# One decoder step: low parts of w_o and of two up pairs by an adding DMA, and two padding PSUM tiles

## The chip, the cores and the metric

The kernel runs on one core of a Trainium2 chip. The metric is the device time of one execution in microseconds (us); lower is better. The kernel before takes 888.28 us (median of 3 runs, 888.14 to 888.34).

## The reference

One layer of a decoder on two groups of tokens, 512 new ones and 8 sequences of 8, so 576 tokens of width 1024, all in float32:

```python
xn = rms_norm(h, g_mix)
z = xn @ w_in                      # 1024 x 6144: b, c, hc, v, gate_a, gate_b
ya = gated_short_conv(b, c, hc) @ w_out_conv
yb = multiscale_pool(v) @ w_pool * pool_scale    # 4 groups, windows 2, 4, 8, 16
h = h + (gate_a * ya + gate_b * yb) @ w_o
hn = rms_norm(h, g_mlp)
h = h + square(relu(hn @ w_up)) @ w_down         # 1024 -> 4096 -> 1024
gp = sigmoid(rms_norm(h, g_ple) @ w_ple_gate)
h = h + gp * (p @ w_ple_proj)
y = rms_norm(h, g_final)
```

It also returns the last rows of the convolution's and of the pooling's input.

## The kernel before, in words

**Precision.** Every operand of a matmul is split in two float32r tiles: `hi`, the value rounded, and `lo`, what is left. A product of two operands is three matmuls: hi by hi, lo by hi and hi by lo (`mm`, line 104, and `quarter`, line 382). The usual split (`split`, line 87) takes one ScalarE operation for `hi` (line 93) and one VectorE operation, value minus `hi`, for `lo` (line 94).

**Weights.** A weight comes in parts of 128 x 512, 256 KB each. SyncE's queue loads a part into one of 8 `raw` tiles (`raw_tile`, line 126). Its `hi` and `lo` go to the pool `wsp`, which has NF = 7 slots for each, so a part can be split when the part seven places ahead of it has been multiplied. One list, `order`, holds all parts in the order of use, and `Stream.take` keeps loads about 6 parts ahead of the splits and splits up to 7 parts ahead of TensorE. A part of w_o or of the pooling is used by 24 matmuls, a quarter of an up pair by 12.

**Adding parts.** A `Part` made with `adding=True` gets its low part in another way (lines 140 to 149): ScalarE writes `hi` (line 145), ScalarE writes `lo` = -`hi` (line 146), and GpSimd's queue issues a DMA that loads the same weight once more and adds it to `lo` (line 147). Before the change that is so for the parts of w_in and w_pool in the last three pooling groups, 16 parts in all.

**Up pairs.** The products of w_in and w_up with 512 by 512 corners are done in pairs of output blocks, with seven products of quarters where eight would be plain. A pair's eight entries in the list are the forms a, s2, s0, s1, b, (a of the next pair), d, s3. The quarters a, b and d are loaded as they are. The sums need more DMAs on GpSimd's queue: for s1 and s0 a loaded `raw` tile gets a second quarter added to it by a DMA (line 164), which first waits for the load. s2 is a sum on VectorE (line 184) of s1's tile and a; s3 another (line 186) with b. Both are issued in VectorE's stream, so VectorE stops there until the DMA of line 164 has landed.

**Stages around the change.** (1) Pooling, lines 662 to 733: for group 3, 2, 1, 0 two products of 48 matmuls, window sums on VectorE (lines 694 to 724), a split, and one group later `merge` (line 673): two products of 24 matmuls, `t` = PSUM x scale x gate (line 679), plus the mixer's other branch (line 681), a split into `merged`. (2) w_o, lines 748 to 765: eight products of 48 matmuls; the first two are opened together by `two_products` and take the groups' results in the order 2 to 7, then 0 and 1. Each product is added to x (line 755), scaled (line 758), and after every second one `hg.add` makes differences (lines 429 to 432) and splits. (3) The first up block: its first pair is opened late: four quarters run over three of the four operands (36 matmuls) while the last operand is still made, and the rest follows. Then come the pairs 1, 2 and 3.

**PSUM.** In the pooling `psump` has 4 tiles of two banks (line 664). As built, the 16 products take the banks 0-1, 6-7, 4-5, 2-3 in turn, so the last merge's two products lie in 4-5 and 2-3. The pool `banks` that follows (line 743) has 6 tiles of one bank and hands them out first as 0, 5, 4, 3, 2, 1: the first w_o product takes banks 0 and 5. With `reuse_waits="tile"` a tile waits only for those older tiles whose bytes it takes. The banks are handed out while the planner runs, from a list of free ones, so a tile more can shift who gets which.

**Order.** In stages 2 and 3 the matmuls are kept in the order of the program (`pinned`). All other engines' instructions are ordered by a planner, which plays the program through with its own costs and on each engine issues what is ready and comes first in the program. Once built, each engine's queue is fixed: an instruction that waits holds up all behind it, on GpSimd's queue DMA issues and additions of squares (line 329) alike.

Of the kernel before, what the change touches and what calls it, by code (L numbers as in the profile page):

```python
# [7 lines left out]
F32 = mybir.dt.float32  # L8
F32R = mybir.dt.float32r
AF = mybir.ActivationFunctionType  # L10
ALU = mybir.AluOpType

P = 128
D = 1024
NJ = D // P
# [3 lines left out]
NH = 2  # L19
# [17 lines left out]
KH = D // 2  # L37
NQ = NJ // 2
# [4 lines left out]
def tile_hybrid_step(ctx: ExitStack, tc: tile.TileContext, x, pt, vecs, rc, ident, sconv, spool, w_first, w_in,  # L43
                     w_pool, w_oc, w_o, w_up, w_down, w_pg, w_pp,
                     y_out, ncp, npp, ncs, nps):
    nc = tc.nc
# [5 lines left out]
    wsp = ctx.enter_context(tc.tile_pool(name="wsp", bufs=NF))  # L52
# [8 lines left out]
    psum = pool("psumx", 1, space=bass.MemoryType.PSUM)  # L61
# [21 lines left out]
    def as32(ap):  # L83
        return ap.bitcast(F32)
# [41 lines left out]
    def raw_tile(ap):  # L126
        raw = wraw.tile([P, KH], F32, tag="raw", name="raw")
        nc.sync.dma_start(raw, ap)
        return raw

    class Part:

        def __init__(self, ap, resident=False, adding=False):
            self.ap, self.resident, self.adding = ap, resident, adding
# [3 lines left out]

        def split(self):
            if self.adding:  # L140

                n = self.ap.shape[1]
                hi = wsp.tile([P, KH], F32R, tag="w", name="hi")[:, :n]
                lo = wsp.tile([P, KH], F32R, tag="wl", name="lo")[:, :n]
                nc.scalar.copy(hi, self.raw[:, :n])
                nc.scalar.mul(lo, as32(hi), -1.0)
                nc.gpsimd.dma_start(lo, self.ap, accum_op=ALU.add)
                self.raw = None
                return hi, lo
            pool, tag = (acts, "act") if self.resident else (wsp, "w")  # L150
            w = split(self.raw, [P, KH], pool, tag)
            self.raw = None
            return w
# [11 lines left out]
            return raw  # L165

    class Form:
        def __init__(self, pair, name):
            self.pair, self.name = pair, name

        def load(self):
            p, name = self.pair, self.name
# [6 lines left out]

        def split(self):  # L180
            p, name = self.pair, self.name
            if name == "s2":
                p.rs2 = tmp.tile([P, KH], F32, tag="s", name="s2", bufs=2)
                nc.vector.tensor_tensor(out=p.rs2, in0=p.rs1, in1=p.ra, op=ALU.add)  # L184
            elif name == "s3":
                nc.vector.scalar_tensor_tensor(
                    out=p.rs2, in0=p.rs2, scalar=-1.0, in1=p.rb, op0=ALU.mult, op1=ALU.subtract)
            return split(p.rs2 if name == "s3" else getattr(p, "r" + name), [P, KH], wsp, "w")
# [30 lines left out]
    def unit(ap, adding=False):  # L219
        return [Part(ap[:, i:i + KH], adding=adding) for i in range(0, ap.shape[1], KH)]  # L220

    order = []
    order += unit(w_in[NJ + NQ]) + unit(w_in[2 * NJ + NQ]) + unit(w_in[NQ])

    def forms(pairs, between=(), after=()):

        out = [Form(pairs[0], "a")]
        for q, p in enumerate(pairs):
            out += [Form(p, n) for n in ("s2", "s0", "s1", "b")]
            out += [Form(pairs[q + 1], "a")] if q + 1 < len(pairs) else list(between)  # L230
            out += [Form(p, n) for n in ("d", "s3")]
        return out + list(after)

    for q in range(1, NQ):
# [9 lines left out]
        order += unit(w_pool[g + 1], True) if g < 3 else []  # L244
    halved = [i + h * NQ for i in range(NQ) for h in range(2)]
    for j in halved:
        order += unit(w_o[j])
    for b in range(NFB):
        order += forms([Pair(w_up[b * NJ + q], w_up[b * NJ + NQ + q]) for q in range(NQ)])
        for j in range(NJ):  # L250
            order += unit(w_down[b * NJ + j])
    for i in range(2):
# [14 lines left out]
    for j in range(NJ):  # L267
# [4 lines left out]
        raw = wraw.tile([P, KH], F32, tag="raw", name="fraw")  # L272
# [17 lines left out]
    for j in range(NJ):  # L290
        if j == 0:
            hi, lo = (acts.tile([P, NH, HT], F32R, tag="act", name=n) for n in ("hi", "lo"))
            for h in range(NH):
                nc.scalar.mul(hi[:, h], xs[j][:, h], v(G_MIX, j))
                nc.vector.scalar_tensor_tensor(
                    out=lo[:, h], in0=xs[j][:, h], scalar=v(G_MIX, j), in1=as32(hi[:, h]),
# [218 lines left out]
    for u in range(3):  # L515
        for k in (NJ - 2, NJ - 1):
            first_step(k, u)
            if u == 1:
                r = stat.spread(range(3 * (k - NJ + 2), 3 * (k - NJ + 3)))
# [128 lines left out]
    gates, where, tag = mix, keep, "keep"  # L648
    pairs_of(NQ, xo, corner, finish)
    for j in range(NJ):  # L650
        ps = product(stream.take(2), ya_in)
# [3 lines left out]
    gates, where, tag = [None] * NJ, acts, "act"  # L655
# [7 lines left out]
    tmp = pool("tmpp", 8)  # L663
    psum = pool("psump", 4, space=bass.MemoryType.PSUM)
    banks = None
    sp = tmp.tile([P, NJ, DB, PB], F32, tag="sp", name="sp", bufs=1)
    nc.sync.dma_start(sp, spool)
    npp_t = tmp.tile([P, NJ, PB], F32, tag="npp", name="npp_t", bufs=1)
# [16 lines left out]
    for g, w in reversed(list(enumerate(WINDOWS))):  # L685
        pooled = []
        for i in range(2):
            j = 2 * g + i
            ps = product(stream.take(2), xg)
# [5 lines left out]
                out=e[:, PB:PE_].rearrange("p (h t) -> p h t", h=NH),  # L695
                in0=prompt(ps), in1=prompt(r1), op=ALU.mult)
            nc.vector.tensor_tensor(
                out=es[:, :, PB:].rearrange("p (h b) t -> p h b t", h=NH),
# [3 lines left out]
            s, d = e, 1  # L702
            while d < w:
                q = tmp.tile([P, PEXT], F32, tag="ext", bufs=4, name="q")
                lo = 2 * d - 1
                nc.vector.tensor_tensor(  # L706
                    out=q[:, lo:], in0=s[:, lo:], in1=s[:, lo - d:PEXT - d], op=ALU.add)
                s, d = q, 2 * d
            pl = tmp.tile([P, NH, HT], F32, tag="t", name="pl")
            nc.vector.scalar_tensor_tensor(  # L710
                out=prompt(pl), in0=s[:, PB:PE_].rearrange("p (h t) -> p h t", h=NH),
# [3 lines left out]
                out=sample(pl),  # L715
# [9 lines left out]
                out=pl[:, 0, :f], in0=head[:, :f], in1=e[:, PB:PB + f], op=ALU.subtract)  # L725
# [18 lines left out]
    psum = pool("psumm", 1, space=bass.MemoryType.PSUM)  # L744
# [7 lines left out]
    for x, j in enumerate(halved):  # L752
        ps = opened[x] if x < 2 else product(stream.take(2), merged)
# [14 lines left out]
    for b in range(NFB):  # L768
# [29 lines left out]
        for j in range(NJ):  # L798
            if j == 0:
                two = two_products(sq, halved)  # L800
            if j < 2:
                ps = two[j]
            else:
                ps = product(stream.take(2), sq)
# [158 lines left out]
```

## Time and profile before

| | us |
|---|---|
| median of 3 runs | 888.28 |
| the profiled execution | 886.94 |
| its span, first to last instruction | 885.1 |
| TensorE busy | 867.9 (98%) |
| VectorE busy | 594.1 (67%) |
| ScalarE busy | 426.5 (48%) |
| GpSimd busy | 139.5 (16%) |

The mean granted clock is 0.994 of full speed; it is 1.00 in all stretches around the change. A row of a timeline gives start, duration, engine, line, operation, what is written and read, how many instructions of a kind are merged, and in brackets the engine's idle time before it with what ended it. Matmuls overlap in the timeline: each shows about 0.29 us, while the next starts about 0.13 us after it. A matmul's start is therefore the better clock.

### The profile page before, as it was taken

The numbers are of one execution on the slowest core, as the hardware profiler recorded it, in microseconds if no ns is written. First come the engines' busy times: TensorE is split into PE (matmuls) and PEld (weight loads), VectorE is DVE, ScalarE is ACT, GpSimd is POOL, SyncE is SP. The second block draws the span as 40 slices with busy tenths as digits, with TensorE's granted clock in tenths as the row PEclk, the third lists the DMA queues.
The fourth block names the chain that finished last, engine by engine and source line by source line (L and its number), as shares of the span: only waits on it lengthen the run. The fifth ranks groups of instructions, "written<-read, shape, count | busy, mean of one in ns | idle before, by whom it ended". The sixth has DMA issues, their size and how long they took to land.

```text
span 885.1 us, 16776 instructions
## 1 busy us (share of the span) xinstructions
PE 867.9 (98%) x6506; PEld 863.5 (98%) x6506; DVE 594.1 (67%) x1063; ACT 426.5 (48%) x754; POOL 139.5 (16%) x176
## 2 busy tenths in 40 slices
PE   8999999999999999999899999999999999999995
PEld 8999999999999999899899999999999999999995
DVE  7997797974358599768873248535763377687454
ACT  8653343652135555355674247512762167546332
POOL 4212112100010242032200010011001010021353
PEclk9999999999999999999999999999999999999997
DMA  8636546644454776554444454254544454323012
GB/s 261 155 113 148 132 131 159 154 131 116 103 130 133 194 160 134 179 132 107 121 154 116 104 135 128 96 139 101 144 132 117 107 135 132 96 85 108 1 38 71
DMA packets 62160, 111.25 MB, mean 126 GB/s; under 512 B 7296, under 2 KB 11008, under 8 KB 62080
## 3 DMA queue, kind: packets, MB, share of 16 engines
q1 hardware_dynamic: 50992, 90.21, 32.0%
q0 software_dynamic: 10944, 19.93, 14.4%
q8 instruction: 51, 0.84, 0.4%
q14 instruction: 29, 0.24, 0.1%
q10 hardware_dynamic: 144, 0.03, 0.0%
HBM read 107.16 MB, written 2.99 MB: 124 GB/s over the span
## 4 chain that ended last, share of the span: by engine, by line
PE 84%; DVE 9%; issue 3%; DMA 2%; ACT 1%; SPq 0%; POOL 0%; DVEq 0%; POOLq 0%; ACTq 0%
PE b L67 76%; PE psg L67 6%; DVE lo L94 2%; DVE q L706 2%; DMA raw<-w_up 2%; PE psn L340 1%; DMA xin<-x 1%; PE psn L367 1%; ACT hi L93 1%; DVE pl L710 1%; DVE t L679 1%; DVE e L694 0%; DVE t L681 0%; PE ps L67 0%; DVE xall L755 0%
## 5 line engine op out<-in xcount | busy, mean ns | idle before, releaser
L67 PE MATMUL b<-hi 128*128 128x288 f32 x1832 | 461.9, 296 | 4.3 <-DVE t L679 1.6
L67 PE MATMUL b<-lo,hi 128*128 128x288 f32 x1832 | 460.4, 295 | 1.2 <-DVE lo L94 1.1
L67 PE MATMUL b<-hi,lo 128*128 128x288 f32 x1832 | 460.6, 295 | 0.6 <-DVE lo L94 0.6
L67 PEld LDWEIGHTS b<-hi 128*128 128x128 f32 x1832 | 317.6, 188 | 6.7 <-DVE t L679 1.8
L67 PEld LDWEIGHTS b<-lo,hi 128*128 128x128 f32 x1832 | 317.6, 188 | 1.8 <-DVE lo L94 1.6
L67 PEld LDWEIGHTS b<-hi,lo 128*128 128x128 f32 x1832 | 317.5, 188 | 0.9 <-DVE lo L94 0.8
L93 ACT CAST hi<-raw 128x512 fp32r<-128x512 f32 x288 | 177.0, 621 | 266.3 <-PE b L67 253.8
L94 DVE TENSOR_TENSOR lo<-raw,hi 128x512 fp32r<-128x512 f32 x288 | 202.8, 708 | 102.4 <-ACT hi L93 98.2
L164 POOL DMA_DIRECT2D raw<-w_up x32 | 28.1, 878 | 334.5 <-DMA raw<-w_up 151.7
L329 POOL TENSOR_TENSOR sq<-sq 128x576 f32<-128x576 f32 (+2 forms) x32 | 41.6, 1301 | 112.1 <-ACT sq L323 63.4
L93 ACT CAST hi<-s 128x512 fp32r<-128x512 f32 x60 | 37.0, 618 | 45.9 <-PE b L67 41.3
L94 DVE TENSOR_TENSOR lo<-s,hi 128x512 fp32r<-128x512 f32 x60 | 41.2, 688 | 20.3 <-ACT hi L93 18.9
L164 POOL DMA_DIRECT2D raw<-w_in x28 | 24.4, 870 | 183.7 <-DVE lo L94 71.5
L184 DVE TENSOR_TENSOR s<-raw 128x512 f32<-128x512 f32 x30 | 20.7, 690 | 45.5 <-DMA raw<-w_up 28.9
L67 PE MATMUL psg<-hi 128*128 128x320 f32 (+1 forms) x128 | 38.1, 298 | 0.0
L67 PE MATMUL psg<-lo,hi 128*128 128x320 f32 (+1 forms) x128 | 37.9, 296 | 0.0
L67 PE MATMUL psg<-hi,lo 128*128 128x320 f32 (+1 forms) x128 | 37.9, 296 | 0.0
L67 PE MATMUL ps<-lo,hi 128*128 128x288 f32 x160 | 34.4, 296 | 0.0
L67 PE MATMUL ps<-hi 128*128 128x288 f32 x160 | 34.2, 296 | 0.1
L67 PE MATMUL ps<-hi,lo 128*128 128x288 f32 x160 | 34.2, 296 | 0.0
L94 DVE TENSOR_TENSOR lo<-g,hi 128x576 fp32r<-128x576 f32 x32 | 26.3, 834 | 6.6 <-ACT hi L93 6.6
L811 DVE TENSOR_TENSOR acc<-b,acc 128x288 f32<-128x288 f32 x48 | 19.8, 450 | 15.1 <-PE b L67 15.1
(132 smaller groups left out, 803.4 us busy)
## 6 DMA issues: line engine op xcount, KB each, us to landing
raw<-w_in SPq DMA_DIRECT2D x104, 256.0 KB, 3.0
raw<-w_up SPq DMA_DIRECT2D x80, 256.0 KB, 2.9
raw<-w_down SPq DMA_DIRECT2D x64, 256.0 KB, 2.9
raw<-w_up POOLq DMA_DIRECT2D x32, 256.0 KB, 4.3
raw<-w_in POOLq DMA_DIRECT2D x28, 256.0 KB, 4.6
raw<-w_oc SPq DMA_DIRECT2D x16, 256.0 KB, 2.8
raw<-w_o SPq DMA_DIRECT2D x16, 256.0 KB, 3.5
raw<-w_pg SPq DMA_DIRECT2D x16, 256.0 KB, 2.9
```

The lines of the kernel that those rows point to most:

```text
L67: i = nc.tensor.matmul(*args, **kw)
L93: nc.scalar.copy(hi, src)
L94: nc.vector.tensor_tensor(out=lo, in0=src, in1=as32(hi), op=ALU.subtract)
L164: nc.gpsimd.dma_start(raw, y, accum_op=ALU.add)
L184: nc.vector.tensor_tensor(out=p.rs2, in0=p.rs1, in1=p.ra, op=ALU.add)
L329: nc.gpsimd.tensor_tensor(out=self.parts[0], in0=self.parts[0], in1=sq, op=ALU.add)
L340: nc.tensor.matmul(sums[:, i:i + 1], a[:, h, c:c + m], ones32[:, 0:1], start=k == 0, stop=k == len(self.parts) - 1)
L367: nc.tensor.matmul(self.ps[:, h, c:c + m], self.y[:, i:i + 1].broadcast_to([m, P]), idt[:m, :m], start=True, stop=True)
L679: nc.vector.scalar_tensor_tensor(out=t, in0=halves(ps), scalar=v(P_SCALE, j), in1=gates[j], op0=ALU.mult, op1=ALU.mult)
L706: nc.vector.tensor_tensor(out=q[:, lo:], in0=s[:, lo:], in1=s[:, lo - d:PEXT - d], op=ALU.add)
L710: nc.vector.scalar_tensor_tensor(out=prompt(pl), in0=s[:, PB:PE_].rearrange("p (h t) -> p h t", h=NH), scalar=1.0 / w, in1=e[:, PB:PE_].re ...
L811: nc.vector.tensor_tensor(out=accs[j][:, h], in0=ps[h], in1=accs[j][:, h], op=ALU.add)
```

## The change

The adding split becomes a function, `split_adding`, and serves more weights: all 16 parts of w_o, and of the first up block's pairs 0 and 1 the quarters a, b and d, 6 in all. And the pooling allocates two PSUM tiles ahead of its first product; VectorE writes one column into each.

```diff
+    def split_adding(raw, ap):
+        n = ap.shape[1]
+        hi = wsp.tile([P, KH], F32R, tag="w", name="hi")[:, :n]
+        lo = wsp.tile([P, KH], F32R, tag="wl", name="lo")[:, :n]
+        nc.scalar.copy(hi, raw[:, :n])
+        nc.scalar.mul(lo, as32(hi), -1.0)
+        nc.gpsimd.dma_start(lo, ap, accum_op=ALU.add)
+        return hi, lo
...
     class Form:
...
         def split(self):
             p, name = self.pair, self.name
+            if self.adding and name in ("a", "b", "d"):
+                return split_adding(getattr(p, "r" + name), getattr(p, name))
...
-    def forms(pairs, between=(), after=()):
+    def forms(pairs, between=(), after=(), adding=0):
-        out = [Form(pairs[0], "a")]
+        out = [Form(pairs[0], "a", adding > 0)]
         for q, p in enumerate(pairs):
-            out += [Form(p, n) for n in ("s2", "s0", "s1", "b")]
+            out += [Form(p, n, q < adding) for n in ("s2", "s0", "s1", "b")]
...
     for j in halved:
-        order += unit(w_o[j])
+        order += unit(w_o[j], True)
     for b in range(NFB):
-        order += forms([Pair(w_up[b * NJ + q], w_up[b * NJ + NQ + q]) for q in range(NQ)])
+        order += forms([Pair(w_up[b * NJ + q], w_up[b * NJ + NQ + q]) for q in range(NQ)], adding=0 if b else 2)
...
     psum = pool("psump", 4, space=bass.MemoryType.PSUM)
     banks = None
+    for _ in range(2):
+        nc.vector.memset(psum.tile([P, NH, 512], F32, tag="ps", name="pad")[:, 0, :1], 0.0)
```

## Rows read from the trace of the kernel before

**Rows 1.** The page's first part: busy time of each engine, share of the span, instructions.

```profile
PE 867.9 (98%) x6506; PEld 863.5 (98%) x6506; DVE 594.1 (67%) x1063; ACT 426.5 (48%) x754; POOL 139.5 (16%) x176
```

**Rows 2.** The chain of waits in order of time: start, us, what. One long stretch of matmuls without a stall.

```profile
456.21 354.39 PE b L67 x2664
```

**Rows 3.** Stretches: from:to, length, then busy us (instructions) of PE, PEld, DVE, ACT, POOL, granted clock, DMA share, GB/s. Most of the pooling, its end, w_o, and the first up pairs.

```profile
300.00:340.00 40.00, 40.00 (x302) 40.00 (x302) 31.72 (x58) 21.21 (x42) 14.74 (x23) 1.00 0.86 184
344.00:363.00 19.00, 17.32 (x125) 16.40 (x124) 18.82 (x37) 8.90 (x17) 0.00 (x0) 1.00 0.34 103
361.00:414.00 53.00, 51.42 (x383) 51.21 (x384) 38.67 (x60) 24.62 (x42) 11.54 (x10) 1.00 0.47 133
414.00:441.00 27.00, 24.21 (x172) 22.73 (x171) 22.60 (x39) 18.98 (x34) 5.89 (x5) 1.00 0.51 133
```

**Rows 4.** The timeline of TensorE where the pooling's last merge (ps) gives way to w_o (b).

```profile
358.36 0.43 PE L67 MATMUL ps<-hi,lo 128*128 128x288 f32 x2
358.85 0.79 PE L67 MATMUL ps<-hi 128*128 128x288 f32 x4
359.64 0.53 PE L67 MATMUL ps<-lo,hi 128*128 128x288 f32 x2
360.01 0.42 PE L67 MATMUL ps<-hi,lo 128*128 128x288 f32 x2
360.27 0.42 PE L67 MATMUL ps<-lo,hi 128*128 128x288 f32 x2
360.53 0.43 PE L67 MATMUL ps<-hi,lo 128*128 128x288 f32 x2
361.01 0.40 PE L67 MATMUL b<-hi 128*128 128x288 f32 x1
362.98 0.41 PE L67 MATMUL b<-hi 128*128 128x288 f32 x1 [1.56 <-DVE t L679]
```

**Rows 5.** The timeline of TensorE in the first up pair, when the last operand is due. Ten matmuls start from 418.79 to 422.00.

```profile
418.79 0.29 PE L67 MATMUL b<-hi,lo 128*128 128x288 f32 x1
...
419.96 0.40 PE L67 MATMUL b<-lo,hi 128*128 128x288 f32 x1 [0.40 <-DVE lo L94]
...
421.37 0.40 PE L67 MATMUL b<-lo,hi 128*128 128x288 f32 x1 [0.75 <-DVE lo L94]
...
422.74 0.40 PE L67 MATMUL b<-hi 128*128 128x288 f32 x1 [0.45 <-ACT g L441]
...
424.31 0.29 PE L67 MATMUL b<-hi,lo 128*128 128x288 f32 x1
```

**Rows 6.** The timeline of TensorE between the pairs 1 and 2. Thirteen matmuls start from 437.64 to 439.93.

```profile
437.64 0.29 PE L67 MATMUL b<-hi,lo 128*128 128x288 f32 x1
438.38 0.37 PE L67 MATMUL b<-hi 128*128 128x288 f32 x1 [0.45 <-DVE g L463]
...
440.88 0.37 PE L67 MATMUL b<-hi 128*128 128x288 f32 x1 [0.66 <-ACT hi L93]
```

**Rows 7.** The timeline of VectorE at the end of the pooling. `lo<-raw,hi` are low parts of w_o.

```profile
354.87 0.68 DVE L94 TENSOR_TENSOR lo<-raw,hi 128x512 fp32r<-128x512 f32 x1
...
360.84 0.68 DVE L94 TENSOR_TENSOR lo<-raw,hi 128x512 fp32r<-128x512 f32 x1
361.44 0.75 DVE L94 TENSOR_TENSOR lo<-t,hi 128x576 fp32r<-128x576 f32 x1
362.11 0.81 DVE L679 SCALAR_TENSOR_TENSOR t<-ps,vec,ga 128x576 f32<-128x576 f32 x1
```

**Rows 8.** The timeline of VectorE from w_o to the third up pair. L184 is the sum s2, L755 adds a w_o product to x; the `lo<-raw,hi` at 414.69 and 416.18 are those of b of pair 0 and of a of pair 1.

```profile
395.88 0.69 DVE L184 TENSOR_TENSOR s<-raw 128x512 f32<-128x512 f32 x1 [5.59 <-DMA raw<-w_up]
...
414.69 0.68 DVE L94 TENSOR_TENSOR lo<-raw,hi 128x512 fp32r<-128x512 f32 x1
416.18 0.69 DVE L94 TENSOR_TENSOR lo<-raw,hi 128x512 fp32r<-128x512 f32 x1 [0.81 <-ACT hi L93]
416.78 0.82 DVE L755 TENSOR_TENSOR xall<-b,xall 128x288 f32<-128x288 f32 x2
...
433.83 0.69 DVE L184 TENSOR_TENSOR s<-raw 128x512 f32<-128x512 f32 x1 [2.54 <-DMA raw<-w_up]
```

**Rows 9.** ScalarE: the group of the adding parts' negative copies (count, busy us, mean ns), and two rows of the timeline: the high parts of a of pair 1 and d of pair 0, and the scaling after the last w_o product.

```profile
L146 ACT ACTIVATE lo<-hi 128x512 fp32r<-128x512 f32 x16 | 10.1, 633 | 0.5
...
415.54 1.12 ACT L93 CAST hi<-raw 128x512 fp32r<-128x512 f32 x2
417.63 0.78 ACT L758 ACTIVATE gx<-xall,vec 128x576 f32<-128x576 f32 x1 [0.97 <-DVE xall L755]
```

**Rows 10.** GpSimd's queue: the adding DMAs of line 147, by the view of that line (duration of the issue min/median/max in ns, and the time from issue to landing), and two issues of line 164 in the timeline.

```profile
L147 POOL DMA_DIRECT2D lo<-w_in x12: 858/865/867, 294.8 to 335.1; - x12
...
DMA to landing us min/median/max: 4.0/5.2/7.9
...
420.33 0.86 POOL L164 DMA_DIRECT2D raw<-w_up  x1 [8.06 <-DMA raw<-w_up]
...
428.48 0.86 POOL L164 DMA_DIRECT2D raw<-w_up  x1 [7.29 <-DMA raw<-w_up]
```

**Rows 11.** The DMA view of 290 to 345 us, in which GpSimd's queue issues 16 adding DMAs: packets, MB, share of 16 engines.

```profile
q0 software_dynamic: 2304, 4.20, 49.4%
```

**Rows 12.** The timeline of VectorE where the pooling begins: the last read of a PSUM bank of the stage before, of bank 4.

```profile
296.45 0.46 DVE L494 TENSOR_TENSOR g<-b,u 128x288 f32<-128x288 f32 x1 [0.34 <-PE b L67]
```

More of the change, by code (lines that the diff above doesn't have):

```diff
@@ L140, in split @@
             if self.adding:
[L142 to L149, printed above, removed]
+                raw, self.raw = self.raw, None
+                return split_adding(raw, self.ap)
             pool, tag = (acts, "act") if self.resident else (wsp, "w")
@@ L167, in tile_hybrid_step, with __init__ @@
     class Form:
-        def __init__(self, pair, name):
-            self.pair, self.name = pair, name
+        def __init__(self, pair, name, adding=False):
+            self.pair, self.name, self.adding = pair, name, adding
         def load(self):
@@ L223, in tile_hybrid_step @@
     order += unit(w_in[NJ + NQ]) + unit(w_in[2 * NJ + NQ]) + unit(w_in[NQ])
-    def forms(pairs, between=(), after=()):
-        out = [Form(pairs[0], "a")]
+    def forms(pairs, between=(), after=(), adding=0):
+        out = [Form(pairs[0], "a", adding > 0)]
         for q, p in enumerate(pairs):
-            out += [Form(p, n) for n in ("s2", "s0", "s1", "b")]
-            out += [Form(pairs[q + 1], "a")] if q + 1 < len(pairs) else list(between)
-            out += [Form(p, n) for n in ("d", "s3")]
+            out += [Form(p, n, q < adding) for n in ("s2", "s0", "s1", "b")]
+            out += [Form(pairs[q + 1], "a", q + 1 < adding)] if q + 1 < len(pairs) else list(between)
+            out += [Form(p, n, q < adding) for n in ("d", "s3")]
         return out + list(after)
```

## The prediction

> **What bounds the kernel now.** I read the busy times first, then the chain of waits, then TensorE's timeline at the places where its rate falls, and last the engine that each stall names. TensorE is busy for 98% of the span [rows 1]. Its natural pace comes from the longest stretch of the chain: 354.39 us for 2664 matmuls, 0.133 us each [rows 2]. The change adds and removes no matmul, so all it can win is time in which starts lie further apart than that, at the places it touches. There are three.
>
> 1. End of the pooling. From 358.36 to 362.98 are 4.62 us, in which 15 matmuls start (2 + 4 + 2 + 2 + 2 + 2 + 1), worth 2.00 us: 2.62 us lost [rows 4]. The largest piece, a wait of 1.56 us, names VectorE's `t`, the read of the last merge's first product. The reader should see why that is late: VectorE works 18.82 of 19.00 us in this stretch [rows 3], and low parts of w_o stand in its queue between the links of the merge's chain [rows 7].
> 2. First up pair. From 418.79 to 422.74 are 3.95 us with ten matmuls, worth 1.33: 2.62 us lost [rows 5]. The last w_o product ended 42 matmuls (36 + 6) before 418.92, at about 413.3. Its addition to x starts only at 416.78, because the low parts of b and of the next a stand before it, the second waiting 0.81 us for ScalarE [rows 8]. From there the scaling at 417.63 [rows 9], the differences and splits run in series.
> 3. Between the pairs 1 and 2. From 437.64 to 440.88 are 3.24 us with 13 matmuls, worth 1.73: 1.51 us lost [rows 6]. VectorE stood 2.54 us before its sum s2 at 433.83, which waited for a DMA of line 164 [rows 8].
>
> Together 6.75 us, the most that can be won.
>
> **The change part by part.** *Low parts.* Each of the 22 parts takes a subtraction of about 0.68 us off VectorE [rows 7, 8]: 15 us in all, worth only what stands on the path at the three places. Each adds a negative copy of 0.633 us on ScalarE [rows 9], an issue of 0.865 us on GpSimd's queue and 4.0 to 7.9 us, median 5.2, until the data has landed [rows 10]. So a low part is ready 0.63 + 0.87 or less + 5.2, about 6 to 6.5 us after its high part instead of about 0.7.
>
> ScalarE gains 22 x 0.633 = 14 us. It works 24.62 of 53.00 us in w_o and 18.98 of 27.00 in the first pairs [rows 3], so there is room; the cost is in order, at most two copies (1.3 us) ahead of an operation on the path.
>
> The DMA engines: 49.4% of a 55 us stretch for 16 adding DMAs is 1.70 us of all engines each [rows 11]. About ten more fall into the 53 us of w_o and five into the 27 us after it: the shares go from 0.47 and 0.51 to about 0.79 and 0.82. From 300 to 340 us, with the adding DMAs of the pooling, the share is 0.86 and TensorE has no gap [rows 3]. So I cost the traffic at nothing, with up to 1.7 us per transfer that happens to run beside one that is waited for.
>
> The Trainium skill bears on the latency (DMA: Bandwidth & Descriptors, section on the anatomy of one DMA on the SWDGE path): it fits 2.0 us plus bytes over 436e3, which for 256 KB is an estimate of 2.6 us. The trace disagrees: no adding DMA landed in less than 4.0 us [rows 10], and the sums here go by 5.2. With 2.6 every low part below would be in time, and the forecast would be 1 us lower.
>
> *Place 1 after the change.* VectorE loses the low parts at 354.87 and 360.84 and those before; the earlier ones gain little, since the chain waits for TensorE's products anyway. So `t` comes 2 x 0.62, about 1.3 us earlier, plus a little backlog: I take a gain of 1.5 us. The low end is 0, if another link is late; the high end the whole 2.62.
>
> *The padding.* Two tiles more turn the cycle of banks by two, if it stays a cycle: the last merge's products then lie in 0-1 and 6-7 instead of 4-5 and 2-3. The first w_o product takes 0 and 5. So its wait would move from its second matmul to its first, worth nothing (one matmul, 0.13 us). The cycle may break, since the planner may give back a pad's banks early; then neither bank may be taken and the rest of place 1 can go. Or the pooling's first product gets bank 4 and must wait for VectorE's read at 296.45 to 296.91 [rows 12] where today it follows at once: up to 0.75 us lost. I count the pads at 0, from -0.75 to +1.0. The two writes of one column are each shorter than any row here and lie where VectorE has gaps.
>
> *Place 2 after the change.* The two low parts before the addition to x are gone, with the wait of 0.81: 0.68 + 0.69 + 0.81 = 2.2 us. Raw tiles of w_o come free after ScalarE's read instead of VectorE's later one, so the loads and sums behind the wait of 5.59 us at 395.88 [rows 8] can start earlier too. Against it stands ScalarE: the scaling (417.63) comes after the high parts at 415.54 [rows 9], and two negative copies may slip in, 1.3 us. Of 2.62 I take 1.5, from 0.3 to 2.6. What is late next are the new low parts themselves. That of the next a is needed at 424.31 [rows 5] and its high part is made at 415.54: 8.8 us, of which the DMA takes 6 to 6.5. With all three gains in front of it some 2.4 us of slack would be used up, so more than about 2.5 us cannot come from here.
>
> *Place 3 after the change.* The sum s2 waits for a DMA, not for VectorE. Lighter VectorE work only makes that wait longer; earlier raw tiles shorten it; more traffic (one transfer, 1.7 us) lengthens it. I take 0, from -2 to +1.5.
>
> Sum: 1.5 + 0 + 1.5 + 0 = 3.0 us. The profiled execution took 886.94 us, 1.84 more than its span, so 883.9 for such an execution. It lies 1.34 below the median of the runs shown, 888.28; on that scale the forecast is 885.3.
>
> **The rivals.** *All three stalls go.* For it: VectorE is named directly or one step back at each. Against it: place 3 waits for a DMA. Price: 888.28 - 6.75 = 881.5.
>
> *The wait only changes its name.* The chain at place 1 is bound by TensorE's own products, at place 2 by ScalarE's added copies or by the landing of the new low parts. For it: the margin of 8.8 against 6.5 us. Against it: ScalarE's share. The gain is then about half of one place's 1.5, 0.7: 887.6. A change whose pads leave the bank wait as it is belongs here.
>
> *GpSimd's queue holds up the low parts (slower).* The queue is in order, and the DMA issues of line 164 wait in it for their loads: 8.06 us before 420.33 and 7.29 before 428.48 [rows 10]. If the planner puts the adding DMA of the next a, ready at about 416.8, behind the issue of 420.33, it is issued at 421.2 and lands 5.2 later, at 426.4, where 424.31 is needed: TensorE is then 2.1 us later than before, and the gains ahead are swallowed, 888.28 + 2.1 = 890.4. It decides when the planner expects the load before ScalarE's copy. Against it: in the trace that load lands only at about 420, well after the copy would be ready, and if the planner sees it so too, it issues the copy's DMA first.
>
> **How the numbers follow.** Forecast 885.3, own range 883.0 to 886.4: 0.50. All stalls go: 0.11. The wait changes its name: 0.25. GpSimd's queue: 0.14. About 0.2% or 1.8 us is what a measurement of this kernel can tell from no change, so the first two are faster: 0.61. The third is mostly within it, a few hundredths on either side: same 0.25. The fourth, slower than 890.1: 0.14. The range reaches from all the stalls gone to just short of the last rival: 881.5 to 889.8.
>
> **What would show each step.** Right: after the change no `lo<-raw` of w_o on VectorE, 38 issues by the new function on GpSimd (16 + 22), the start of w_o within 1.3 us of the last merge's matmul, the addition of the last w_o product within 1 us of its end, and the stall after 418 below 1.2 us. Wrong: idle TensorE that names the new low parts or ScalarE; a wait of GpSimd for a load just before an adding issue; a sum s2 that lands later than before relative to its pair; a gap at 296 us where the pooling begins. The prediction fails as a whole if VectorE turns out not to be what was late, or if the planner's new order moves work at places the change does not touch.

## The result, and the profile after

The changed kernel takes 891.01 us (median of 18 runs) beside 887.50 of the kernel before on the same chip: ratio 1.0040, interval 1.0028 to 1.0053. It is slower by 3.5 us, where 3.0 us less was forecast, and it lies above the range. The profiled execution took 893.18 us, its span 891.4 (before: 886.94 and 885.1).

What was to be taken off VectorE was taken off. First the page's busy times, which answer to [rows 1]:

```profile
PE 871.9 (98%) x6506; PEld 867.6 (97%) x6506; DVE 580.9 (65%) x1043; ACT 438.4 (49%) x776; POOL 158.4 (18%) x198
```

VectorE fell by 13 us, ScalarE rose by 12, GpSimd by 19. Then the stretches of [rows 3], and two short ones to which I come back (columns as there):

```profile
344.00:363.00 19.00, 18.90 (x139) 18.21 (x137) 17.06 (x34) 11.29 (x23) 5.52 (x8) 1.00 0.83 188
361.00:414.00 53.00, 52.16 (x388) 51.73 (x389) 29.22 (x44) 30.70 (x52) 20.72 (x21) 1.00 0.85 200
414.00:441.00 27.00, 23.64 (x160) 22.46 (x159) 17.64 (x33) 20.91 (x38) 8.25 (x10) 0.94 0.78 166
424.31:427.72 3.41, 3.02 (x12) 2.87 (x13) 2.61 (x5) 2.53 (x5) 1.10 (x2) 0.50 0.89 139
444.80:448.20 3.40, 3.25 (x13) 3.28 (x14) 3.40 (x8) 0.63 (x2) 0.00 (x0) 0.50 0.22 79
```

The DMA shares of the last two long stretches, 0.85 and 0.78, came out near the forecast 0.79 and 0.82. Yet from 414 to 441 there are 160 matmuls instead of 172, and part of the stretch runs at half clock.

Both traces hold all 6506 matmuls in the same order, so the start of the same matmul can be compared. The difference, after minus before, is a running account of where the time went:

| up to the matmul that started before at | it starts after at | difference | change in this stage |
|---|---|---|---|
| 296.12 (last one ahead of the pooling) | 297.24 | +1.12 | +1.12 |
| 360.01 (end of the pooling) | 362.04 | +2.03 | +0.91 |
| 363.48 (w_o running) | 364.43 | +0.95 | -1.08 |
| 424.31 (end of place 2) | 428.38 | +4.07 | +3.12 |
| 437.64 (ahead of place 3) | 441.72 | +4.08 | 0 |
| 449.02 (behind place 3) | 456.15 | +7.13 | +3.05 |

After that the difference stays until the final norm, where the span's end makes up 0.8. The first 1.12 us belong to this one execution: a stretch at half clock near 25 us, in code that the change doesn't touch. Other kernels whose code there is the same showed it too (below). The rest is the pads, place 1, place 2 and place 3. The sizes are those of these two executions: their times lie 6.2 us apart, the medians 3.5, since the one after is 2.2 us above its median and the one before 0.6 below. TensorE's timeline there:

```profile
297.24 0.29 PE L67 MATMUL b<-hi,lo 128*128 128x288 f32 x1
298.18 0.50 PE L67 MATMUL ps<-hi 128*128 128x288 f32 x2 [0.64 <-DVE g L499]
...
363.82 0.50 PE L67 MATMUL b<-hi 128*128 128x288 f32 x2 [0.83 <-DVE t L687]
...
419.98 0.30 PE L67 MATMUL b<-hi,lo 128*128 128x288 f32 x1
422.51 0.40 PE L67 MATMUL b<-hi 128*128 128x288 f32 x1 [2.23 <-ACT hi L93]
...
441.72 0.29 PE L67 MATMUL b<-hi,lo 128*128 128x288 f32 x1
444.95 0.58 PE L67 MATMUL b<-hi 128*128 128x288 f32 x1 [2.94 <-DVE g L468]
```

The first two rows are the pads: the pooling's first product takes the bank that is read last, and waits for the read (before, the last read was that of [rows 12], of a bank that the product didn't take). The third is place 1, with one wait of 0.83 instead of 1.56 us [rows 4]. The other two pairs are new long stalls at places 2 and 3. Both name VectorE or ScalarE, neither names a low part. The reader should go one step back, to VectorE's own waits. They answer to [rows 8]; L189 is the sum s2, L763 the addition of a w_o product to x, L468 a read of PSUM that place 3 waits for:

```profile
397.26 0.69 DVE L189 TENSOR_TENSOR s<-raw 128x512 f32<-128x512 f32 x1 [11.23 <-DMA raw<-w_up]
397.87 0.82 DVE L763 TENSOR_TENSOR xall<-b,xall 128x288 f32<-128x288 f32 x2
...
417.12 1.54 DVE L763 TENSOR_TENSOR xall<-b,xall 128x288 f32<-128x288 f32 x4
421.78 0.76 DVE L434 TENSOR_TENSOR gt<-gx 128x576 f32<-128x576 f32 x1 [3.12 <-ACT gx L766]
...
439.02 0.69 DVE L189 TENSOR_TENSOR s<-raw 128x512 f32<-128x512 f32 x1 [3.54 <-DMA raw<-w_up]
...
439.99 2.57 DVE L94 TENSOR_TENSOR lo<-s,hi 128x512 fp32r<-128x512 f32 x1
442.49 1.94 DVE L94 TENSOR_TENSOR lo<-g,hi 128x576 fp32r<-128x576 f32 x1
444.36 0.44 DVE L468 TENSOR_TENSOR g<-b,u 128x288 f32<-128x288 f32 x1
```

VectorE, relieved of 22 low parts, stands 11.23 us for the sum s2 of pair 1, twice as long as before (5.59), and 3.54 for the next one (2.54). What waits behind it is the addition of a w_o product that TensorE finished long ago.

The reader should not take the longer wait for a later sum. The sum starts 1.38 us later than before (397.26 against 395.88), and the matmuls of w_o run 0.95 later by the account, so against TensorE it is 0.4 us late. The wait doubled because VectorE stands there earlier, from 386.03 instead of 390.29, and because the order of its queue has changed. Before, the addition of the fourth w_o product stood ahead of the sum, and the differences right behind it; now that addition stands behind the sum, and the differences wait for it and for its scaling:

```profile
388.88 0.81 DVE L755 TENSOR_TENSOR xall<-b,xall 128x288 f32<-128x288 f32 x2
...
396.48 0.75 DVE L429 TENSOR_TENSOR gt<-gx 128x576 f32<-128x576 f32 x1
```

```profile
399.53 0.76 DVE L434 TENSOR_TENSOR gt<-gx 128x576 f32<-128x576 f32 x1 [0.85 <-ACT gx L766]
```

From the sum to the differences pass 2.27 us instead of 0.60. So of the 2.1 us by which the differences are late against TensorE, 1.7 come from the order and 0.4 from the sum.

The transfers beside the sum did become slower. The DMA view of 380 to 398 us, of the kernel after:

```profile
q0 software_dynamic: 1119, 2.03, 68.8%
...
lo<-w_o POOLq DMA_DIRECT2D x5, 256.0 KB, 7.8
raw<-w_up SPq DMA_DIRECT2D x4, 256.0 KB, 6.3
```

and of the kernel before (packets, MB, share; then issues, KB each, median us to landing):

```profile
q0 software_dynamic: 432, 0.79, 25.1%
...
raw<-w_up SPq DMA_DIRECT2D x4, 256.0 KB, 3.3
```

Five adding DMAs of w_o lie there, and the plain loads of w_up, which the sums of line 167 (line 164 before) wait for, take 6.3 instead of 3.3 us (median). The chain of waits of the kernel after shows the load and the sum's DMA in a row (start, us, what):

```profile
384.93 4.06 DMA raw<-w_up
388.99 3.92 issue
392.93 4.31 DMA raw<-w_up
```

From the load's issue on SyncE to the sum's on GpSimd pass 8.0 us, then 4.3 until it lands; before they were 3.9 and 5.9, from an issue at 386.01. The load started 1.1 us earlier than before, which is why so much of its slowness doesn't show in the sum. The Trainium skill (DMA: Bandwidth & Descriptors, section "Issuing engines are not separate DMA queues") says that DMAs started by SyncE and by GpSimd end on the same 16 engines and interleave. This trace agrees: the loads on SyncE's queue became slower by transfers that only GpSimd issued.

### The profile page after: what moved, and what is told of

Its sections match the earlier page's. It is cut to its first block, busy times and chain, and to the rows that moved or that the text cites. A ratio compares the mean times of both kernels' runs of the same rounds, so it can differ in the third digit from the quotient of the medians.

```text
span 891.4 us, 16824 instructions
## 1 busy us (share of the span) xinstructions
PE 871.9 (98%) x6506; PEld 867.6 (97%) x6506; DVE 580.9 (65%) x1043; ACT 438.4 (49%) x776; POOL 158.4 (18%) x198
## 4 chain that ended last, share of the span: by engine, by line
PE 89%; DVE 4%; DMA 3%; issue 2%; ACT 2%; POOL 0%; SPq 0%; DVEq 0%; ACTq 0%; POOLq 0%
PE b L67 75%; PE ps L67 6%; PE psg L67 6%; DMA raw<-w_up 3%; DVE lo L94 1%; PE psn L345 1%; PE psn L372 1%; DVE gt L436 0%; ACT hi L136 0%; DMA xin<-x 0%; ACT gx L766 0%; ACT sq L328 0%; DVE xall L763 0%; DVE gt L434 0%; DVE t L687 0%
## 5 line engine op out<-in xcount | busy, mean ns | idle before, releaser
L93 ACT CAST hi<-raw 128x512 fp32r<-128x512 f32 x266 | 163.7, 621 | 258.5 <-PE b L67 247.2
L94 DVE TENSOR_TENSOR lo<-raw,hi 128x512 fp32r<-128x512 f32 x266 | 186.8, 706 | 95.7 <-ACT hi L93 91.9
L189 DVE TENSOR_TENSOR s<-raw 128x512 f32<-128x512 f32 x30 | 20.7, 690 | 58.6 <-DMA raw<-w_up 39.7
L94 DVE TENSOR_TENSOR lo<-s,hi 128x512 fp32r<-128x512 f32 x60 | 44.0, 734 | 16.9 <-ACT hi L93 15.4
L136 ACT CAST hi<-raw 128x512 fp32r<-128x512 f32 x38 | 23.4, 616 | 13.0 <-PE b L67 7.2
```

Of the source, the lines that this page charges most:

```text
L93: nc.scalar.copy(hi, src)
L94: nc.vector.tensor_tensor(out=lo, in0=src, in1=as32(hi), op=ALU.subtract)
L136: nc.scalar.copy(hi, raw[:, :n])
```

## The experiments

Three theories. T: the new transfers make the sums s2 late, VectorE stands for them in order, and what is queued behind on VectorE stops TensorE. ScalarE: the negative copies stand ahead of operations on its path. Landing: the operands themselves come late by the transfers, whoever waits. Ratios are to the kernel before, with intervals.

**The parts one by one.** Two pads alone (e1_pads):

```diff
+    for _ in range(2):
+        nc.vector.memset(psum.tile([P, NH, 512], F32, tag="ps", name="pad")[:, 0, :1], 0.0)
```

> The two padding tiles alone, all low parts as before. Bank theory: the pooling's first product now takes bank 4 and waits for VectorE's last read, a gap of 0.7 to 0.8 us at 296 us, and the wait at the start of w_o moves from the second matmul to the first, so the time grows by 0.8 us (ratio 1.001). Rival, that the pads also free the start of w_o: gap at 296 us gone again by a gain of 1 us or more at 361 us, ratio 0.999.

1.0010 (0.9993 to 1.0027): no difference that can be told. In its trace the two rows of the pads are

```profile
300.12 0.50 PE L67 MATMUL ps<-hi 128*128 128x288 f32 x2 [0.64 <-DVE g L499]
...
366.92 0.50 PE L67 MATMUL b<-hi 128*128 128x288 f32 x2 [2.10 <-DVE t L687]
```

so the bank wait at the pooling's start is theirs (0.80 us from the matmul before it, less its own pace), and the start of w_o still waits for `t`. This execution, too, had half clock near 25 us, 6.8 us of it.

The 16 parts of w_o alone (e2_wo): `unit(w_o[j], True)` and nothing else.

> w_o's low parts by adding DMA alone, no pads, up pairs as before. If the loss of the whole change comes from the up quarters (ScalarE's copies ahead of the last scaling, their DMAs beside the sums): place 1 wins 1 to 1.5 us, the stalls at 419 and 438 stay at 2.6 and 1.5 us, ratio 0.998 to 0.999. If it comes from w_o's DMAs that fill the DMA engines between 383 and 395 us and delay the sums: VectorE's wait for the sum s2 near 396 us grows from 5.6 to about 11 us and the ratio is 1.002 to 1.004.

0.9981 (0.9969 to 0.9994), a gain: place 1 won 1.3 us, place 2 got its new wait of 2.21 us, place 3 did not stall. VectorE's wait for the sum grew to 10.97 us, as the second theory had it, and yet the kernel is faster.

The six up quarters alone (e3_up): `adding=0 if b else 2` and nothing else.

> The six up quarters by adding DMA alone, no pads, w_o as before. Theory of the up quarters: the scaling of the last w_o product waits behind two negative copies, the stall after 418 us grows to 4 us or more and one stretch at half clock follows, ratio 1.002 to 1.004. Theory of w_o's traffic: VectorE's wait near 396 us stays at 5.6 us, the stalls stay as they are, ratio 0.999 to 1.001.

1.0023 (1.0004 to 1.0041), a loss, but not at the place expected: place 2 lost 2.4 us, no more than before, and TensorE waited 2.17 us for L468 at place 3. Both together without the pads (e4_wo_up):

> The whole change without the pads. If the pads cost 0.75 us and nothing else, this is 0.7 to 0.8 us faster than the whole change, ratio to before 1.003. If the pads shift more than that (the planner's order behind them), it differs from the whole change by over 2 us.

1.0026 (1.0012 to 1.0041). So the pads are not the cause; the gain of w_o is eaten by the up quarters and by what both do at place 2. In this run's trace place 2 lost 3.8 us by the account and place 3 only 0.15, against 3.1 and 3.05 in the whole change: the loss at place 3 isn't in every trace.

**Transfers or ScalarE's copies?** The six quarters with the copies but without the DMA (e5_copies), and with the DMA but the copies on VectorE (e6_vcopies):

```diff
         nc.scalar.mul(lo, as32(hi), -1.0)
-        nc.gpsimd.dma_start(lo, ap, accum_op=ALU.add)
```

```diff
-        nc.scalar.mul(lo, as32(hi), -1.0)
+        nc.vector.tensor_scalar(out=lo, in0=as32(hi), scalar1=-1.0, scalar2=None, op0=ALU.mult)
         nc.gpsimd.dma_start(lo, ap, accum_op=ALU.add)
```

> The six up quarters as in the run of the up quarters alone, but the adding DMA is left out: ScalarE still writes the high part and the negative copy, which is then used as the low part (that part of the computation is left out). Theory (the six transfers, 1.7 us of all engines each, delay the sum of line 167 that s2 waits for between the pairs 1 and 2): without them the stall at 438 to 442 falls from 2.33 us to 1.5 or less, no stretch at half clock follows it, and the time is that of the kernel before or less, 886.5 to 888.5. Rival (ScalarE's six added copies, 0.63 us each, stand ahead of operations on the path): the stall stays above 2 us and the time stays near 889.3.

> The six up quarters with the adding DMA, but VectorE writes the negative copies in place of ScalarE; nothing is left out. So ScalarE has the work of the kernel before, and the six transfers are there. Theory (transfers): the stall between the pairs 1 and 2 stays at about 2.3 us, the DMA share of 414 to 426 stays near 0.89, and the time is 889 to 890.5. Rival (ScalarE's copies): back to 888.5 or less.

Without the transfers 0.9982 (0.9966 to 0.9998), with them and without ScalarE's copies 1.0032 (1.0012 to 1.0051). The clean pair is e3_up and e5_copies, the same copies with and without the DMAs: the copies cost nothing, the transfers (with their issues on GpSimd) cost. e6_vcopies shows less, since the place is another than expected: TensorE waits for a low part itself,

```profile
431.25 0.40 PE L67 MATMUL b<-hi,lo 128*128 128x288 f32 x1 [2.74 <-DMA lo<-w_up]
```

and GpSimd's queue shows why: its issue at 424.14 stands behind one that waited for a load.

```profile
423.60 0.86 POOL L170 DMA_DIRECT2D raw<-w_up  x1 [6.33 <-DMA raw<-w_up]
424.14 1.21 POOL L141 DMA_DIRECT2D lo<-w_up  x1
```

That is the rival "GpSimd's queue holds up the low parts", here and, for 0.7 us, in e11_s2pool below.

**Which parts of w_o?** The first 8 (e7_first8) and the last 8 (e10_late8):

```diff
-        order += unit(w_o[j], True)
+        order += unit(w_o[j], j in halved[:4])
```

(`halved[4:]` for the last 8.)

> Only the first 8 parts of w_o add by DMA, up quarters and pads as before. Theory (the gain of w_o comes at the end of the pooling, where the first parts are split; the later parts only crowd the queues at 383 to 395 us, and the jam there makes the last addition to x late): the start of w_o loses about 1.0 us as with all 16, the first up pair at most what it lost before, 2.6, in pieces below 1.5 us and with no stretch at half clock after them; 885.0 to 886.2. Rival (place 2 has its long wait from somewhere else than the later parts): a single wait above 2 us at 418 to 423 remains, 886.4 or more.

> Only the last 8 parts of w_o add by DMA, the first 8 as before: the complement of the run with the first 8. Theory (the first 8 bring the gain, the last 8 the loss): the start of w_o loses about 2 us as before the change, the wait of s2 on VectorE before 395 grows to 8 us or more, the wait above 2 us in the first up pair is there with a half clock after it, and the time is 888.5 to 890.5, slower than before. Rival (the loss needs all 16, by the sheer number of transfers): place 2 as before and 887.5 to 888.5.

First 8: 0.9953 (0.9936 to 0.9970), 884.85 us. Last 8: 1.0026 (1.0009 to 1.0044). The first are split beside the pooling's end, where VectorE is the bottleneck [rows 3]; the last add transfers at 380 to 395, and of the two runs only theirs has the addition of the fourth product behind the sum, as the whole change has. VectorE's stop for s2 of pair 1 in the two, first 8 first:

```profile
393.83 0.69 DVE L189 TENSOR_TENSOR s<-raw 128x512 f32<-128x512 f32 x1 [4.93 <-DMA raw<-w_up]
```

```profile
399.32 0.69 DVE L189 TENSOR_TENSOR s<-raw 128x512 f32<-128x512 f32 x1 [8.73 <-DMA raw<-w_up]
```

One thing in e10_late8 was not expected: a further 2.17 us in the pooling's last merge, for a high part on ScalarE. It wasn't followed up; by the account it cost 2.1 us, place 2 5.1.

**The rest of place 1.** All 16 parts, no pads in the pooling, and the first product of w_o on banks that the last merge doesn't use (e8_banks: `psumm` opened ahead of `banks`, one pad tile in `banks`).

> All 16 parts of w_o add by DMA, no pads in the pooling; instead the PSUM pools after the pooling are laid out so that the first product of w_o takes banks 6 and 7, which the last merge doesn't use (pool psumm opened ahead of banks, and one pad tile in banks). Theory (what is left of the stall at the start of w_o, 1.0 us, is the wait for the read of the last merge's product): it goes, 885.0 to 885.8 if nothing else changes. Rival (behind the bank wait stands another, for merged operands or weights): the loss near 360 us stays at 0.7 or more, 886.0 to 886.8.

0.9993 (0.9981 to 1.0005): the loss at the start of w_o went from 0.77 to 0.50, place 2 stalled by 2.21 as with all 16 but with 6.8 us at half clock behind it instead of 3.4, and 0.87 us were newly lost near 821, where a late stage begins. The median, 888.28 us, is above both expected ranges: nothing won.

**The half clock.** All 16 parts, and 16 matmuls that nobody reads ahead of the stalled one (e9_filled).

```diff
+                    for _ in range(filled):
+                        matmul(spare, w[0][:, :P], op.f["b11"][0][0], start=True, stop=True)
                 quarter(pa, w, op.f["b11"], rest, False, True)
```

> All 16 parts of w_o add by DMA, as in that run, and ahead of the matmul that waits in the first up pair (a loss of 2.21 us before 420.12) TensorE does 16 matmuls whose result nobody reads, 2.1 us at its own pace; what the kernel computes is unchanged. Theory (the stretch of 3.4 us at half clock from 422 on follows from TensorE standing still): no half clock after 420, each of some 14 matmuls at 0.13 instead of 0.24 us, so 1.6 us less than the 886.4 of all 16: 884.5 to 885.3, although the operand comes no earlier. Rival (the half clock has nothing to do with the stall, or comes from the smaller waits that follow): the stretch stays, 886.2 to 886.8.

The half clock at place 2 was gone, as expected. First all 16 parts as they were, then filled:

```profile
422.05:425.45 3.40, 3.13 (x12) 2.98 (x13) 2.60 (x6) 2.53 (x5) 0.22 (x1) 0.50 0.53 82
```

```profile
420.00:424.00 4.00, 1.91 (x10) 1.23 (x10) 3.26 (x7) 2.31 (x6) 0.86 (x1) 1.00 0.49 112
424.00:428.00 4.00, 4.00 (x28) 3.77 (x29) 3.96 (x8) 2.79 (x6) 0.00 (x0) 1.00 0.22 47
```

The time was not: 0.9987 (0.9974 to 0.9999). By the account of matmul starts place 2 cost 2.6 us with the filling and 2.7 without: at full clock TensorE reached the next link earlier and waited 0.96 us more for it. So the half clock hid in the chain there, and the expected 1.6 us were wrong. Place 3, calm in the trace of all 16, stalled here by 2.20; the profiled execution was the slowest of its 12 (889.00, median 887.39).

**Whose wait is it?** The decisive edit adds and removes no transfer and moves only the sum s2 from VectorE to GpSimd, for chosen pairs of the first block:

```diff
-                nc.vector.tensor_tensor(out=p.rs2, in0=p.rs1, in1=p.ra, op=ALU.add)
+                e = nc.gpsimd if p.pool else nc.vector
+                e.tensor_tensor(out=p.rs2, in0=p.rs1, in1=p.ra, op=ALU.add)
```

The first try, on all 16 parts of w_o, moved the sum of pair 0 (e11_s2pool), which was a wrong reading of mine: the long wait is pair 1's.

> All 16 parts of w_o add by DMA, and the sum s2 of the first up pair is made by GpSimd instead of VectorE, so that the wait of 11 us for the DMA of line 167 stands on GpSimd's queue. Theory (that wait on VectorE's queue makes the additions to x late and with them the last operand): VectorE goes on at 384 to 395, the long wait of 2.2 us in the first up pair falls below 1 us with no half clock after it, 884.3 to 885.5. Rival (the later additions wait for something else, the products or ScalarE; or GpSimd's later issues of adding DMAs come late by the wait and TensorE stands for a low part): a loss of 2 us or more remains between 384 and 424, 886 or more.

1.0015 (1.0001 to 1.0029). GpSimd's sum held back the DMA behind it, and VectorE stood longer than ever:

```profile
399.12 0.69 DVE L191 TENSOR_TENSOR s<-raw 128x512 f32<-128x512 f32 x1 [17.11 <-DMA raw<-w_up]
```

TensorE then also stood at 394 and 415 us, for 0.84 and 1.47. Here the sum is truly late, by 4.3 us against TensorE, and place 2 lost 7.3 us by the account: as a dose it speaks for T. With the sum of pair 1 instead (e12_s2of1):

> All 16 parts of w_o add by DMA, and the sum s2 of the up pair 1 (not pair 0, as in the run before: the wait of 11 us belongs to pair 1) is made by GpSimd, so that its wait for the DMA of line 167 stands on GpSimd's queue; the last two adding DMAs of w_o are queued behind it. Theory (VectorE's stop for this sum makes the later additions to x, and with them the last operand of the first up pair, late): VectorE goes on at 384 to 395, the loss of 2.21 us ahead of 420 falls below 1 us and no half clock follows, 884.3 to 885.8. Rival (the additions are late for another reason, or a low part of w_o that now waits on GpSimd's queue stops TensorE between 384 and 415): a loss of 2 us or more remains, 886.2 or more.

0.9952 (0.9934 to 0.9969), 884.24 us. The DMA is as late as before, but it is GpSimd that waits,

```profile
395.03 1.28 POOL L191 TENSOR_TENSOR s<-raw 128x512 f32<-128x512 f32 x1 [3.22 <-DMA raw<-w_up]
```

and place 2 is gone: no gap above 0.2 us between 362 and 433. The same for the pairs 1 to 3 in the whole change without pads (e13_s2all), for pair 1 alone in the run with the first 8 parts (e14_best), and for the pairs 1 to 3 in the kernel before (e15_before_s2) and in the change as it was (e16_after_s2):

> The whole change without its pads, with the sums s2 of the up pairs 1, 2 and 3 of the first block on GpSimd instead of VectorE. Theory (the up quarters' loss, too, is VectorE standing for such a sum while TensorE waits for what is queued behind it): VectorE reads its banks in time, the loss at 436 to 442 falls below 1 us, and the time is 886.0 to 888.0, against 890.5 for the same with s2 on VectorE. Rival (the operand of the matmul is late in itself, since the transfers are late, whichever engine adds): 889.5 to 891.5, with TensorE waiting for a high or low part of s2 or for a quarter instead.

> The run with the first 8 parts of w_o, plus the sum s2 of pair 1 on GpSimd. In the run with the first 8 VectorE still stood 4.93 us for that sum, and the first up pair lost 0.35 + 0.90 + 0.61 us. Theory: the additions to x come earlier by up to 2 us, the first two of these losses go and some of it is given back between the pairs 1 and 2, where the sum for pair 2 is timed by its DMA: 883.6 to 885.0, at or below the 884.9 of the first 8. Rival (the chain from the last product of w_o on is bound by its own links): no change, 884.5 to 885.5.

> The kernel before, without any part of the change, with the sums s2 of the up pairs 1, 2 and 3 of the first block on GpSimd. If these sums alone stand behind the gain of the last three runs (low parts by DMA then add nothing): 883 to 884.5. If low parts by DMA and the sums each bring their own share (the start of w_o still loses some 2 us here, and VectorE still makes 22 low parts): 885.0 to 886.5, that is a half to two thirds of the way.

> The whole change with its pads, and the sums s2 of the up pairs 1, 2 and 3 of the first block on GpSimd. Theory (the slowdown of the change comes from VectorE standing for those sums, and the pads cost 0.8 us where the pooling begins and give at the start of w_o nothing): the losses at the first up pair and at 436 to 442 fall below 1.3 us each, 883.5 to 885.5, some 6 us below the change as it was. Rival (the pads turn more against it, by moving the order of the queues): 886 or more.

| version | median us | ratio | interval |
|---|---|---|---|
| first 8 parts of w_o | 884.85 | 0.9953 | 0.9936 to 0.9970 |
| w_o and up quarters, s2 on VectorE | 890.49 | 1.0026 | 1.0012 to 1.0041 |
| the same, s2 of pairs 1 to 3 on GpSimd | 883.38 | 0.9952 | 0.9934 to 0.9970 |
| first 8 parts, s2 of pair 1 on GpSimd | 883.08 | 0.9952 | 0.9932 to 0.9972 |
| kernel before, s2 of pairs 1 to 3 on GpSimd | 885.12 | 0.9977 | 0.9963 to 0.9991 |
| the change with its pads, s2 on VectorE | 891.01 | 1.0040 | 1.0028 to 1.0053 |
| the same, s2 of pairs 1 to 3 on GpSimd | 883.45 | 0.9953 | 0.9937 to 0.9970 |

One edit that adds and removes no transfer turns the change from 0.40% slower to 0.47% faster. The sums alone bring 0.23%, the change with them out of the way about as much again. e15 came out within its expected range, e13 2.6 us below the range of its theory, e14 and e16 just below theirs. TensorE's waits from 290 to 450 us, summed by the view of waits, first of the change as it was, then with the sums on GpSimd (us in total, times, longest):

```profile
PE b L67 <- DVE g L468: 2.9, 1, 2.9
PE b L67 <- ACT hi L93: 2.2, 1, 2.2
PE b L67 <- DVE lo L94: 1.1, 2, 0.7
PE b L67 <- DVE t L687: 0.8, 1, 0.8
PE ps L67 <- DVE g L499: 0.6, 1, 0.6
```

```profile
PE b L67 <- DVE g L470: 1.1, 1, 1.1
PE b L67 <- DVE t L689: 0.8, 1, 0.8
PE ps L67 <- DVE g L501: 0.6, 1, 0.6
```

And the DMA engines were busier in the stretch ahead of place 2, not less: 366 to 414 of the change as it was, then of the change with the sums on GpSimd.

```profile
366.00:414.00 48.00, 48.00 (x362) 48.00 (x361) 24.24 (x37) 27.59 (x47) 19.44 (x19) 1.00 0.82 193
```

```profile
366.00:414.00 48.00, 48.00 (x362) 48.00 (x361) 28.22 (x42) 31.52 (x54) 23.70 (x23) 1.00 0.91 204
```

A DMA share of 0.91 without a stall, and no wait of TensorE for a DMA in either list: "landing" is refuted for these places. Of T the second half is shown, that VectorE stands in order for the sum and that what is queued behind it stops TensorE. With the sum on GpSimd the addition of the fourth product runs at once:

```profile
388.21 0.82 DVE L765 TENSOR_TENSOR xall<-b,xall 128x288 f32<-128x288 f32 x2 [3.42 <-PE b L67]
```

The first half, that the new transfers make the sum late, is not what counted at place 2, where the sum was 0.4 us late. The order of VectorE's queue sorts the runs instead. In the seven traces in which the addition of the fourth product stands behind pair 1's sum on VectorE (the change, e2, e4, e8, e9, e10, e11) place 2 lost 2.6 us or more by the account. In the five changed kernels in which it stands ahead (e1, e3, e5, e6, e7) place 2 gained, or lost at most 1.3 with 3.4 us at half clock on the way. This order is fixed when the kernel is built. Why the planner chose it, because VectorE had less to do or because of the transfers in its own costs, no run separates: the 16 parts of w_o with their copies and without their DMAs weren't run.

The versions at the top, 883.1 to 884.9, cannot be told apart, and all beat both kernels.

## Why the prediction was wrong, step by step

**Place 1, gain 1.5.** Right in its mechanism: 1.3 us with the 16 parts alone, 1.1 with the pads.

**Pads, 0 (from -0.75 to +1.0).** The waits fit a cycle turned as foreseen: the first w_o matmul waits now, no longer the second (the banks themselves don't show in a trace). The named cost at the pooling's start came, too: 0.91 in the account, of which 0.80 is that one gap, a little beyond the bound. Nothing came back at the start of w_o. In medians, 883.45 with and 883.38 without them: nothing that can be measured.

**Place 2, gain 1.5.** This step failed, with its sign: 3.1 us lost. The sentence that was wrong is "the loads and sums behind the wait of 5.59 us at 395.88 can start earlier too". The load did start 1.1 us earlier, but beside the adding DMAs it took 7.5 instead of 3.3 us, and the sum came 0.4 us late against TensorE. Above all the step took VectorE's queue as it was, with less in it. In the queue of the changed kernel VectorE stands for the sum from 386.03 on, 11.23 us, and an addition to x that had been ahead of the sum is behind it, which made the differences 2.1 us late. The prediction named a new order by the planner as a way to fail, but only for places that the change doesn't touch. The loss stands in two parts: 2.4 us until the matmul of 423.30 (3.34 after its 419.96 of [rows 5], against 0.95 in w_o), and 0.7 more by the half clock that follows. The named risk, ScalarE's two copies ahead of the scaling, also came true: in the change as it was,

```profile
419.28 0.63 ACT L137 ACTIVATE lo<-hi 128x512 fp32r<-128x512 f32 x1
...
420.45 0.63 ACT L137 ACTIVATE lo<-hi 128x512 fp32r<-128x512 f32 x1
420.99 0.76 ACT L766 ACTIVATE gx<-xall,vec 128x576 f32<-128x576 f32 x1
```

but with w_o alone, with no such copies there, place 2 stalled by 2.21 as well, so it was not what counted.

**Place 3, 0 (from -2 to +1.5).** 3.05 lost in this trace. "More traffic lengthens it" was the right direction: the sum at 439.02 comes 1.1 us later against TensorE than the one at 433.83 [rows 8]. Another 1.4 us are lost between the sum and the read L468 (L463 before) that TensorE waits for. Before, one of the two low parts that stand there was long,

```profile
435.41 2.46 DVE L94 TENSOR_TENSOR lo<-g,hi 128x576 fp32r<-128x576 f32 x1
```

and the other took 0.68 us; now both are long, 2.57 and 1.94, because GpSimd's additions of squares (440.25, 3.57 us for two) run beside both. The half clock behind it makes the remaining 0.6. The Trainium skill (SBUF — State Buffer, section "SBUF: two separate sides") says that a VectorE operation with two inputs from SBUF and a GpSimd operation that reads SBUF exclude each other; the 2.57 and 1.94 agree with it. With the sums on GpSimd both causes go at once (the two low parts take 0.69 and 0.75 in e16_after_s2), so how much each would cost alone isn't separated.

**Traffic at nothing.** The failed term behind place 3, and the smaller part of place 2. The pooling, with a share of 0.86 and no gap [rows 3], was a poor witness. There VectorE has no sum in its queue that waits for a DMA. What a transfer costs isn't the share of the engines but the wait that it prolongs and what stands in line behind it.

**The rivals.** None was the one that came. The fourth, slower, is near in time (890.4 against 891.01) but not by its path: in the change no wait of TensorE names a new low part. "All three stalls go" was, apart from 1.0 us lost at place 1 and 1.2 behind place 2, what the change does once the sums are off VectorE: by the account place 2 then gains 2.4 us, and place 3, with the 1.2 ahead of it, 0.5. GpSimd's queue held up a low part only in e6_vcopies and e11_s2pool.

## What to carry to other kernels

Before adding DMA traffic look on every in-order engine for instructions that already wait for a DMA: a relieved engine doesn't run ahead, it stands in front of the longest of these waits, with everything behind it. After the change look at the order of its queue again, and compare a late operation with TensorE's progress, not with the length of the wait: here the wait doubled while the sum was 0.4 us late. Price a new transfer by the waits it lies beside, not by the mean share of the DMA engines, and move such a wait to a queue in which nothing urgent stands behind it. Then moving work onto DMA paid here: 0.2%, with a DMA share of 0.91 ahead of the first up pair.

## What the runs showed of the hardware

TensorE's granted clock fell from 2.4 to 1.2 GHz in the middle of the kernel, for 3.41 us at a time (6.83 in some runs), after stretches in which it had stood (424.31 and 444.80 above, in a kernel 98% busy). Matmuls then start 0.24 us apart instead of 0.13. The cost by the account was 0.7 and 0.6 us at these two places, since TensorE waited less for the links that followed, and 1.1 near 25 us, where nothing was waited for. It isn't settled when it comes: in e6_vcopies a stall of 2.9 us at 428 was followed by none, and the wait of 1.6 us at the start of w_o by none in the kernel before and by 3.41 us of it in e3_up. The spread goes with it: the 18 runs of the change go from 887.8 us at a mean clock of 0.992 to 894.3 at 0.987.

An adding DMA of 256 KB took 4.3, 5.8 and 9.0 us (least, median, most) to land after the change, against 4.0, 5.2 and 7.9 before [rows 10].
